# The ring of high and low weight halves in a pool of its own at the other end of the partition

## The chip, the core and the metric

The kernel runs on one core of one Trainium2 chip. The metric is the device time of one execution in microseconds. Kernel and reference take the same inputs, one layer, 512 tokens of width 2048, all in float32.

## The reference, cut to what matters

```python
h = rms_norm(x, norm1_g) * (1.0 + sc1) + sh1        # sc1, sh1, g1, ... = silu(c) @ w_ada + b_ada
proj = h @ w_in                                     # 2048 x 7168
o_hg = hgrn2_mixer(hg_q, hg_f, hg_i, hg_g, ...)     # gated linear recurrence, 8 heads
o_sb = stick_breaking_mixer(sb_q, sb_k, sb_v, ...)  # attention, 8 heads
x = x + g1 * (concatenate([o_hg, o_sb]) @ w_out)    # 2048 x 2048
h = rms_norm(x, norm2_g) * (1.0 + sc2) + sh2
gate, up = split(h @ w_ffn_in, 2)                   # 2048 x 11264
x = x + g2 * ((silu(gate) * up) @ w_ffn_out)        # 5632 x 2048
```

Nearly all of the work is in the four large products with `w_in`, `w_out`, `w_ffn_in` and `w_ffn_out`.

## The kernel before

**Three products for one.** The large products use float32 rounded to a shorter form (`F32R`). To keep float32's accuracy each operand is split into a high half, its rounded copy, and a low half, the rest. A product is then three matmuls: high by high, high by low, low by high (`three`, L227, and the same pattern in `product`, `multiply` and `sb_project`). `split` (L212) makes the halves of a weight piece: ScalarE casts the raw weights into `hi`, VectorE subtracts `hi` from the raw weights into `lo`. Both are put ahead of other work by `tc.high_priority`.

**The ring.** The halves go to tiles of pool `wp` (L137) with the tags `hi` and `lo`, three buffers each, 4096 bytes a partition and buffer: 24,576 bytes in all. The same pool holds `raw`, four buffers of 8192 bytes into which SyncE's queue loads the weights from HBM. In the loop over `w_ffn_in`, and after it, every fourth call of `split` takes its pair of tiles from `spare` instead: `hi2` and `lo2` of pool `tp` in the loop (L1095), a part of tile `opsB` in the last stage (L1156).

**Stages.** The program runs through these, mostly one after the other:

- `st`: the first 1024 columns of `w_in`. The weights are the *moving* operand (512 columns); a piece of `hhi` or `hlo`, the halves of h, is the stationary one that LDWEIGHTS loads. 384 matmuls.
- `sbp`: the attention's projections, 8 heads; weights moving, 384 columns, `hhi` or `hlo` stationary. 8 heads x 8 pieces x 24 = 1536 matmuls. Attention itself is interleaved (`zA`, `tA`, `sbo`, ...).
- `hgf`, `hgq`, `hgg`: the recurrence's projections, 8 heads; weights *stationary* out of the ring, `hhi` or `hlo` moving with 512 columns. 8 x 3 x 48 = 1152 matmuls, with the recurrence between them (`l`, `r`, `hgo`, ...).
- `wo`: the product with `w_out`; weights stationary, 512 columns: 15 x 48 = 720 matmuls, and the last output block in two halves of 256 columns, 96 matmuls.
- `ff`: the first two blocks of `w_ffn_in`, 384 matmuls of 256 columns, beside the second normalisation.
- `ffA`, `ffB`, `ffC`: the loop `for f in range(2, FM)` (L1108), 42 rounds. Each round replaces eight block products by seven (a Strassen-like scheme, with sums of weight blocks made by VectorE), each of 24 matmuls of 256 columns with weights stationary (`product`, L908): 42 x 7 x 24 = 7056 matmuls. A piece `ff_3h` is the high half of the third product's weights out of the ring, `ff_3l` the low half; `ff_3hi` and `ff_3lo` are the same out of the spare pair.
- `foA`, `foB`, `foC`: the product with `w_ffn_out` by the same scheme (`multiply`, L1174); weights moving, 512 columns, 1848 matmuls, of which 1344 take them from the ring and 504 from the spare part of `opsB`.

**Where things lie.** A partition has one address range. Pools on the left side are laid out upwards from its low end, one after another; pools with `side="right"` downwards from its top. A pool that closes frees its stretch for the next. No address is written in the kernel: each follows from the pools that are open.

Of the kernel before, what the change touches and what calls it, by code (L numbers as in the profile page):

```python
# [11 lines left out]
F32R = mybir.dt.float32r  # L12
# [5 lines left out]
P = 128  # L18
# [111 lines left out]
def trunk(ctx, tc, a):  # L130
# [4 lines left out]

    const = ctx.enter_context(tc.tile_pool(name="const", bufs=1))
    wp = ctx.enter_context(tc.tile_pool(name="wp", bufs=3))  # L137
    xctx = ctx.enter_context(ExitStack())
    xop = xctx.enter_context(tc.tile_pool(name="xop", bufs=1, side="right"))
    hp = ctx.enter_context(tc.tile_pool(name="hp", bufs=1))  # L140
# [27 lines left out]
    def small_col(base, i=0):  # L168
        return small[:, base + i:base + i + 1]
# [9 lines left out]
    def gemv(w, row, col):  # L179
        V.scalar_tensor_tensor(w, w, 1.0, row, op0=ALU.mult, op1=ALU.mult, accum_out=col)  # L180

    def finish_gain(comp, k0, k1):
        g, base = (gain1, C_N1) if comp == SC1 else (gain2, C_N2)
        V.scalar_tensor_tensor(g[:, k0:k1], mod[:, comp * KT + k0:comp * KT + k1], 1.0, small[:, base + k0:base + k1],
                               op0=ALU.add, op1=ALU.mult)

    def ada(comp, k):
        j = comp * KT + k
        c = slice(j, j + 1)
        gemv(row_load(a["w_ada"][j], f"ada{j}"), cond, mod[:, c])  # L190
        left[comp] -= 1
        if comp == SC1:
            V.tensor_add(mod[:, c], mod[:, c], small_col(C_BADA, j))
            finish_gain(comp, k, k + 1)
        elif not left[comp]:
            all_k = slice(comp * KT, comp * KT + KT)
            V.tensor_add(mod[:, all_k], mod[:, all_k], small[:, C_BADA + comp * KT:C_BADA + comp * KT + KT])
            if comp == SC2:
                finish_gain(comp, 0, KT)
# [12 lines left out]
    def split(r, shape, name):  # L212
        count[0] += 1
        if spare and count[0] % 4 == 0:
            hi, lo = spare[0](shape, name)
        else:
            hi = wp.tile(shape, F32R, tag="hi", name=name + "h")
            lo = wp.tile(shape, F32R, tag="lo", name=name + "l")
        with tc.high_priority(offset=AHEAD):
            S.copy(hi, r)  # L220
            V.tensor_sub(lo, r, hi.bitcast(F32))
        return hi, lo

    def weights(src, shape, name):
        return split(load(src, shape, name), shape, name)
# [60 lines left out]
    for k in range(KT):  # L286
        xk = xo[:, k]
        if k == 0:
            for i in range(2):
                sl = slice(i * 1024, i * 1024 + 1024)  # L290
                gemv(r0[:, sl], cond[:, sl], lead[:, i:i + 1])
            j = SC1 * KT
            V.scalar_tensor_tensor(mod[:, j:j + 1], lead[:, 0:1], lead[:, 1:2], small_col(C_BADA, j), op0=ALU.add, op1=ALU.add)
            finish_gain(SC1, 0, 1)
            whi = wp.tile([P, 1024], F32R, tag="hi", name="wi0h")
            wlo = wp.tile([P, 1024], F32R, tag="lo", name="wi0l")
            for sl in (slice(0, T), slice(T, 2 * T)):
                S.copy(whi[:, sl], w0[:, sl])
                V.tensor_sub(wlo[:, sl], w0[:, sl], whi[:, sl].bitcast(F32))
        else:  # L300
            nc.sync.dma_start(xk, a["x"][:, k])
            ada(SC1, k)
            if k == 2:
                nc.sync.dma_start(cst, a["cst"])
            if k == KT - 1:
                nc.sync.dma_start(ident2, a["cst"][:, 0])
            whi, wlo = weights(a["w_hi"][k], [P, 1024], f"wi{k}")
        gk = gain1[:, k:k + 1]
        S.activation(hhi[:, k], xk, AF.Identity, scale=gk)
        V.scalar_tensor_tensor(hlo[:, k], xk, gk, hhi[:, k].bitcast(F32), op0=ALU.mult, op1=ALU.subtract)  # L310
        if k == 0:
            S.activation(ss1, xk, AF.Square)
        else:
            sq = sb.tile([P, T], F32, tag="qT" if k % 2 else "kT", name=f"sq{k}", bufs=1)
            S.activation(sq, xk, AF.Square)
            V.tensor_add(ss1, ss1, sq)
        for n in range(2):
            for t in range(4):
                ts_ = slice(t * P, t * P + P)
                cs = slice(n * T, n * T + T)  # L320
                out = banks[n * 4 + t]
                PE.matmul(out, hhi[:, k, ts_], whi[:, cs], start=(k == 0), stop=False)
                PE.matmul(out, hhi[:, k, ts_], wlo[:, cs], start=False, stop=False)
                PE.matmul(out, hlo[:, k, ts_], whi[:, cs], start=False, stop=(k == KT - 1))
# [12 lines left out]
    def sb_project(h):  # L337
        ps = [acc(f"sbp{h}_{t}") for t in range(4)]
        for c in range(8):
            if c % 2 == 0:  # L340
                raw = load(a["w_sb"][h, c // 2], [P, 2, 2, 384], f"wsb{h}_{c}")
            whi, wlo = split(raw[:, c % 2], [P, 2, 384], f"wsb{h}_{c}")
            pairs = [(kk, t) for kk in range(2) for t in range(4)]
            if c in (0, 7):
                pairs.sort(key=lambda p: p[1])
            for kk, t in pairs:
                k = 2 * c + kk
                ts_ = slice(t * P, t * P + P)
                out = ps[t][:, 0:384]
                PE.matmul(out, hhi[:, k, ts_], whi[:, kk], start=(k == 0), stop=False)  # L350
                PE.matmul(out, hhi[:, k, ts_], wlo[:, kk], start=False, stop=False)
                PE.matmul(out, hlo[:, k, ts_], whi[:, kk], start=False, stop=(k == KT - 1))
                clock.run()
        clock.until(lambda: h not in reuse or reuse[h] in done)
        if h in (0, 3):
            rows = scr[:, 0:3].rearrange("p a b -> p (a b)").rearrange("p (t c) -> p t c", t=4)
        else:
            rows = sb.tile([P, 4, 384], F32, tag="rows", name=f"rows{h}")
        for t in range(4):
            if t % 2:  # L360
                V.tensor_copy(rows[:, t], ps[t][:, 0:384])
            else:
                S.copy(rows[:, t], ps[t][:, 0:384])
        ready[h] = rows
# [234 lines left out]
    def mtile(src, name, xhi, xlo, out, nk=KT):  # L599
        n = 0  # L600
        raw = load(src, [P, nk, P], name)
        for c0 in range(0, nk, HALF):
            w = min(HALF, nk - c0)
            whi, wlo = split(raw[:, c0:c0 + w], [P, w, P], f"{name}_{c0}")
            for kk in range(w):
                three(out, whi[:, kk], wlo[:, kk], xhi[:, c0 + kk], xlo[:, c0 + kk], n == 0, n == nk - 1)
                n += 1
                clock.run()
# [734 lines left out]
```

## Time and profile before

| | us |
|---|---|
| median of three runs | 2311.63 |
| lowest and highest run | 2308.95, 2312.49 |
| the profiled execution's own time | 2309.45 |
| its span, first to last instruction | 2307.6 |
| PE busy in the span | 2253.1 (98%), 14171 matmuls |
| DVE busy | 1919.5 (83%) |
| ACT busy | 1160.1 (50%) |

PE is TensorE's matmuls, PEld its weight loads, DVE VectorE, ACT ScalarE, SP the queue that issues the transfers. Matmuls overlap in the records, so a busy PE is not yet a PE at its peak. In the rows of stretches below the columns are length, then busy us (x instructions) of PE, PEld, DVE, ACT and POOL, the granted clock, the DMA engines' busy share and GB/s. What tells more than busy time is the distance from the start of one matmul, or weight load, to the start of the next.

### The profile page before, as it was taken

The page shows a single profiled execution, that of the slowest core. Times are in us where ns is not written, and L with a number is a line of the kernel's source. Part 1 is how long each engine was busy: PE and PEld are TensorE (multiplying, and loading weights), DVE is VectorE, ACT ScalarE, POOL GpSimd, SP SyncE. Part 2 cuts the span into 40 slices and gives each one's busy share as a digit, 9 for nine tenths or more (in the row PEclk, how much of TensorE's full clock was granted, in tenths as well). Part 3 has the DMA queues.
Part 4 walks back from the last instruction along what each step waited for, and adds up shares of the span by engine and source line. Part 5 has one row for each costly group of instructions (what it writes and reads, how often), then busy time and mean ns, then how long its engine had stood idle before and what let it go on. Part 6 is the DMA issues. An engine that isn't in the chain of part 4 may idle for free.

```text
span 2307.6 us, 35720 instructions
## 1 busy us (share of the span) xinstructions
PE 2253.1 (98%) x14171; PEld 2049.8 (89%) x14171; DVE 1919.5 (83%) x2570; ACT 1160.1 (50%) x2011; POOL 10.7 (0%) x25
## 2 busy tenths in 40 slices
PE   8999899999999999989999999999999999999998
PEld 6899799888888788989999999999999978878776
DVE  8887779999887864699899988888888777888888
ACT  4326666565656422654445444454545545454443
POOL 0000000000000000000000000000000000000000
PEclk9999999999999999999999999999999999999999
DMA  9886446843322486336555534454544486654553
GB/s 368 314 319 225 166 153 230 305 170 126 110 92 76 155 294 209 111 114 238 206 203 197 209 133 165 142 174 142 174 142 157 177 343 237 219 178 142 183 204 87
DMA packets 114978, 437.69 MB, mean 190 GB/s; under 512 B 9822, under 2 KB 58236, under 8 KB 76796
## 3 DMA queue, kind: packets, MB, share of 16 engines
q1 hardware_dynamic: 114812, 435.42, 53.0%
q8 instruction: 111, 1.82, 0.3%
q14 instruction: 55, 0.45, 0.1%
HBM read 386.61 MB, written 48.77 MB: 189 GB/s over the span
## 4 chain that ended last, share of the span: by engine, by line
PE 79%; DVE 11%; DMA 4%; ACT 3%; issue 3%; SPq 0%; DVEq 0%; ACTq 0%
PE ffA L93 17%; PE ffC L93 9%; PE foA L93 8%; PE sbp L93 8%; PE wo L93 7%; PE ffB L93 4%; PE foC L93 4%; PE st L93 4%; PE hgf L93 4%; PE hgq L93 3%; PE hgg L93 3%; PE foB L93 1%; DVE ada L180 1%; PE l L93 1%; DMA opd<-fhi 1%
## 5 line engine op out<-in xcount | busy, mean ns | idle before, releaser
L180 DVE SCALAR_TENSOR_TENSOR ada<-ada,cond 128x2048 f32<-128x2048 f32 x95 | 216.9, 2286 | 49.0 <-DMA ada<-in_w_ada 49.0
L93 PE MATMUL ffA<-opD,ff_3h 128*128 128x256 f32 x512 | 93.6, 283 | 0.8 <-ACT u L1008 0.8
L93 PE MATMUL ffA<-opB,ff_6h 128*128 128x256 f32 x512 | 93.6, 283 | 0.2 <-ACT a L1008 0.2
L93 PE MATMUL ffC<-opB,ff_7h 128*128 128x256 f32 x512 | 93.5, 283 | 0.0
L93 PE MATMUL ffC<-opC,ff_4h 128*128 128x256 f32 x496 | 90.8, 284 | 0.4 <-ACT c L1008 0.3
L93 PE MATMUL ffB<-opA,ff_2h 128*128 128x256 f32 x496 | 91.3, 284 | 0.0
L93 PE MATMUL ffA<-opC,ff_5h 128*128 128x256 f32 x496 | 90.6, 283 | 0.0
L93 PE MATMUL ffA<-opA,ff_1h 128*128 128x256 f32 x496 | 90.6, 283 | 0.0
L1082 ACT CAST fhi<-forms 128x512 fp32r<-128x512 f32 (+1 forms) x63 | 43.6, 692 | 90.6 <-DMA opd<-fhi 74.1
L93 PEld LDWEIGHTS ffA<-opD,ff_3h 128*128 128x128 f32 x512 | 79.8, 192 | 1.0 <-ACT u L1008 1.0
L93 PEld LDWEIGHTS ffA<-opB,ff_6h 128*128 128x128 f32 x512 | 79.7, 192 | 0.4 <-ACT a L1008 0.4
L93 PEld LDWEIGHTS ffC<-opB,ff_7h 128*128 128x128 f32 x512 | 79.8, 192 | 0.0
L93 PEld LDWEIGHTS ffC<-opC,ff_4h 128*128 128x128 f32 x496 | 77.2, 192 | 0.8 <-ACT c L1008 0.8
L93 PEld LDWEIGHTS ffB<-opA,ff_2h 128*128 128x128 f32 x496 | 77.7, 193 | 0.1
L93 PEld LDWEIGHTS ffA<-opC,ff_5h 128*128 128x128 f32 x496 | 77.3, 192 | 0.0
L93 PEld LDWEIGHTS ffA<-opA,ff_1h 128*128 128x128 f32 x496 | 77.3, 192 | 0.0
L1083 DVE TENSOR_TENSOR forms<-forms,fhi 128x512 fp32r<-128x512 f32 (+1 forms) x63 | 49.0, 778 | 31.0 <-ACT fhi L1082 30.6
L93 PE MATMUL ffA<-opD,ff_3l 128*128 128x256 f32 x256 | 72.5, 283 | 0.0
L93 PE MATMUL ffC<-opB,ff_7l 128*128 128x256 f32 x256 | 72.4, 283 | 0.0
L93 PE MATMUL ffA<-opB,ff_6l 128*128 128x256 f32 x256 | 72.4, 283 | 0.0
L93 PE MATMUL ffB<-opA,ff_2l 128*128 128x256 f32 x248 | 70.3, 284 | 0.0
L93 PE MATMUL ffA<-opA,ff_1l 128*128 128x256 f32 x248 | 70.2, 283 | 0.0
(1644 smaller groups left out, 7759.3 us busy)
## 6 DMA issues: line engine op xcount, KB each, us to landing
ada<-in_w_ada SPq DMA_DIRECT2D x95, 1024.0 KB, 5.0
wfo<-in_w_fo SPq DMA_DIRECT2D x16, 1024.0 KB, 6.0
yraw<-in_w_fo SPq DMA_DIRECT2D x16, 1024.0 KB, 5.1
fix<-in_w_fix SPq DMA_DIRECT2D x14, 1024.0 KB, 5.7
opsA<-opd SPq DMA_DIRECT2D x12, 1024.0 KB, 4.9
opd<-forms SPq DMA_DIRECT2D x44, 256.0 KB, 3.7
opd<-fhi SPq DMA_DIRECT2D x42, 256.0 KB, 4.2
opd<-forms SPq DMA_DIRECT2D x22, 384.0 KB, 6.7
```

Of the source, the lines that this page charges most:

```text
L93: self.engine.matmul(out, lhsT, rhs, **kw)
L180: V.scalar_tensor_tensor(w, w, 1.0, row, op0=ALU.mult, op1=ALU.mult, accum_out=col)
L1082: S.copy(hi, R[:, q])
L1083: V.tensor_sub(R[:, q].bitcast(F32R), R[:, q], hi.bitcast(F32))
```

## The change

The tags `hi` and `lo` leave pool `wp` for a new pool `wt` with three buffers, on the right side and opened before every other pool there. Nothing else is edited.

```diff
@@ -135,6 +135,7 @@
 
     const = ctx.enter_context(tc.tile_pool(name="const", bufs=1))
     wp = ctx.enter_context(tc.tile_pool(name="wp", bufs=3))
+    wt = ctx.enter_context(tc.tile_pool(name="wt", bufs=3, side="right"))
     xctx = ctx.enter_context(ExitStack())
     xop = xctx.enter_context(tc.tile_pool(name="xop", bufs=1, side="right"))
     hp = ctx.enter_context(tc.tile_pool(name="hp", bufs=1))
@@ -214,8 +215,8 @@
         if spare and count[0] % 4 == 0:
             hi, lo = spare[0](shape, name)
         else:
-            hi = wp.tile(shape, F32R, tag="hi", name=name + "h")
-            lo = wp.tile(shape, F32R, tag="lo", name=name + "l")
+            hi = wt.tile(shape, F32R, tag="hi", name=name + "h")
+            lo = wt.tile(shape, F32R, tag="lo", name=name + "l")
         with tc.high_priority(offset=AHEAD):
             S.copy(hi, r)
             V.tensor_sub(lo, r, hi.bitcast(F32))
@@ -292,8 +293,8 @@
-            whi = wp.tile([P, 1024], F32R, tag="hi", name="wi0h")
-            wlo = wp.tile([P, 1024], F32R, tag="lo", name="wi0l")
+            whi = wt.tile([P, 1024], F32R, tag="hi", name="wi0h")
+            wlo = wt.tile([P, 1024], F32R, tag="lo", name="wi0l")
```

In the built programs every engine has the same instructions in the same order, and each waits for the same semaphores at the same values. Only addresses differ. In bytes from the start of the partition:

| tiles | before | now |
|---|---|---|
| constants, `cond`, `small`, `raw` (11,040 to 43,807) | the same | the same |
| ring: `hi` | 43,808 to 56,095 | 204,768 to 217,055 |
| ring: `lo` | 56,096 to 68,383 | 217,056 to 229,343 |
| `hhi`, `ohi`, `opB`, `opsC` | from 68,384 | from 43,808 |
| `hlo`, `olo`, `opC`, `opsB` | from 101,152 | from 76,576 |
| `opA`, `opsA` (and `cst`) | from 133,920 | from 109,344 |
| `opD` | from 166,688 | from 142,112 |
| spare pair `hi2`, `lo2` | 213,984 to 222,175 | 189,408 to 197,599 |
| every other tile | | 24,576 lower |

## Rows read from the trace of the kernel before

**Rows 1.** The page's first part, TensorE: busy us (share of the span) xinstructions.

```profile
PE 2253.1 (98%) x14171; PEld 2049.8 (89%) x14171; DVE 1919.5 (83%) x2570; ACT 1160.1 (50%) x2011; POOL 10.7 (0%) x25
```

**Rows 2.** Stretches st, sbp, hg, wo, ff, loop, fo: us; busy by engine; clock; DMA.

```profile
11.00:101.00 90.00, 89.46 (x383) 73.67 (x384) 80.47 (x118) 39.16 (x53) 0.00 (x0) 1.00 0.95 357
101.00:438.00 337.00, 326.37 (x1898) 312.39 (x1897) 276.13 (x373) 178.48 (x432) 0.00 (x0) 0.98 0.63 226
438.00:768.00 330.00, 327.62 (x1675) 275.23 (x1674) 288.74 (x541) 201.27 (x444) 9.05 (x16) 1.00 0.36 131
768.00:954.00 186.00, 183.31 (x865) 152.05 (x866) 115.49 (x147) 58.89 (x93) 0.00 (x0) 1.00 0.61 212
954.00:1008.00 54.00, 47.61 (x388) 46.74 (x387) 54.00 (x139) 45.01 (x105) 0.00 (x0) 0.99 0.32 110
1008.00:1848.00 840.00, 836.89 (x7037) 835.83 (x7038) 721.02 (x815) 418.92 (x613) 0.00 (x0) 1.00 0.50 174
1848.00:2307.00 459.00, 441.86 (x1933) 353.87 (x1932) 380.47 (x434) 212.69 (x270) 0.00 (x0) 0.99 0.56 198
```

**Rows 3.** Groups by line, TensorE's matmuls of the loop: xcount, busy us, mean ns.

```profile
L93 PE MATMUL ffA<-opD,ff_3h 128*128 128x256 f32 x512 | 93.6, 283 | 0.8 <-ACT u L1008 0.8
L93 PE MATMUL ffA<-opC,ff_5h 128*128 128x256 f32 x496 | 90.6, 283 | 0.0
...
L93 PE MATMUL ffA<-opC,ff_5l 128*128 128x256 f32 x248 | 70.2, 283 | 0.0
...
L93 PE MATMUL ffA<-opC,ff_5hi 128*128 128x256 f32 x176 | 30.5, 276 | 0.0
```

**Rows 4.** Timeline of weight loads in one round of the loop: start us, us, what.

```profile
1401.04 0.31 PEld L93 LDWEIGHTS ffC<-opB,ff_7hi 128*128 128x128 f32 x2
...
1403.77 0.30 PEld L93 LDWEIGHTS ffA<-opC,ff_5h 128*128 128x128 f32 x2
...
1406.64 0.31 PEld L93 LDWEIGHTS ffC<-opC,ff_4h 128*128 128x128 f32 x2
```

**Rows 5.** Chain of waits in the loop, pieces in order: start us, us, what.

```profile
1204.85 2.88 PE ffA L93 x24
1207.73 2.72 PE ffC L93 x24
```

**Rows 6.** The same view, one piece each of st, sbp, hgq, wo, foA.

```profile
19.78 40.35 PE st L93 x178
...
305.49 4.17 PE sbp L93 x24
...
578.60 2.74 PE hgq L93 x12
...
859.83 30.37 PE wo L93 x134
...
1999.78 7.27 PE foA L93 x32
```

**Rows 7.** Chain shares by line in sbp, hg, wo, the loop and fo.

```profile
by line: PE sbp L93 57.2%; issue 4.8%; PE sbo L93 4.7%; DVE ada L180 4.6%; DVE xo L498 2.8%; DVE fix L180 2.2%; DVE I L440 2.1%; PE zA L93 2.1%; DVE L L434 1.9%; PE qkt L98 1.7%; PE tB L98 1.6%; PE zB L93 1.5%; DVE I L441 1.4%; DVE L L439 0
...
by line: PE hgf L93 25.0%; PE hgq L93 23.2%; PE hgg L93 21.8%; PE l L93 5.8%; PE hgo L93 4.8%; PE r L93 2.8%; issue 2.3%; DMA whg0r<-in_w_hg 2.1%; PE b L93 2.0%; DMA ada<-in_w_ada 1.4%; DVE I L440 0.9%; PE hgo L98 0.8%; DVE ada L180 0.8%; P
...
by line: PE wo L93 87.4%; PE wo15h L93 4.6%; issue 2.3%; PE hgo L93 1.2%; ACT wo_0h L220 0.8%; PE l L93 0.7%; PE r L93 0.7%; ACT x L890 0.6%; DVE wo_8l L221 0.6%; PE ssum L93 0.6%; ACT wo_8h L220 0.6%; PE hgo L98 0.3%; DVE olo L801 0.3%; AC
...
by line: PE ffA L93 47.8%; PE ffC L93 23.9%; PE ffB L93 11.9%; issue 2.8%; DMA opd<-fhi 2.3%; DMA ada<-in_w_ada 1.3%; DMA wu23r<-in_w_fi 0.9%; DMA wu8r<-in_w_fi 0.8%; DMA wu5r<-in_w_fi 0.7%; DMA wu6r<-in_w_fi 0.6%; DMA wu9r<-in_w_fi 0.6%; A
...
by line: PE foA L93 42.0%; PE foC L93 21.7%; PE foB L93 4.7%; DVE yraw L1181 3.7%; issue 3.6%; DVE wfo_2l L221 3.5%; DVE T L1181 3.2%; DVE wfo L1245 2.7%; DVE wfo_0l L221 1.9%; ACT wfo_0h L220 1.8%; DVE wfo L1181 1.7%; DVE opsB L221 1.3%; D
```

**Rows 8.** Groups by line, the writes of the halves: xcount, busy us, mean ns, idle.

```profile
L221 DVE TENSOR_TENSOR ff_5l<-ffS,ff_5h 128x1024 fp32r<-128x1024 f32 x31 | 37.8, 1219 | 0.0
L221 DVE TENSOR_TENSOR ff_5lo<-ffS,ff_5hi 128x1024 fp32r<-128x1024 f32 x11 | 13.4, 1219 | 0.0
```

**Rows 9.** Waits of ScalarE in the loop: who waits for what: us, times, longest.

```profile
ACT fhi L1082 <- DMA opd<-fhi: 74.1, 40, 3.8
```

## The prediction

> **What bounds the kernel now.** First the page's busy times: TensorE works through 98% of the span, VectorE through 83% [rows 1]. Then the same by stage: TensorE is busy 836.89 of 840.00 us in the loop over `w_ffn_in`, 327.62 of 330.00 in the recurrence, 183.31 of 186.00 with `w_out` [rows 2]. Only the stretch `ff` (954 to 1008 us) has another engine full, VectorE with 54.00 of 54.00, and `st` runs at a DMA share of 0.95. The granted clock is 1.00 in nearly every stretch, which is 2.4 GHz. So where the loop, `hg` and `wo` stand, the time is the number of matmuls times the distance from one to the next, and whatever moves that distance moves the end.
>
> The built programs differ in nothing but addresses: the same instructions in the same order on every engine, the same waits. The question is therefore narrow: does the time of any instruction hang on where its operands lie? The kernel before holds a test of that. In the loop three of four weight pieces are read out of the ring, at 43,808 to 68,383, and every fourth out of the spare pair, at 213,984 to 222,175. Shape, type, partner and instruction are the same. The groups by line show a matmul out of the ring at 283 ns and one out of the spare pair at 276 ns, whichever of the halves it reads [rows 3]. A record's length is not its price, since matmuls overlap, so I read starts. In one round the 24 weight loads of a spare product, `ff_7hi` and its low half, go from 1401.04 to 1403.77 us, 2.73 us; the 24 of the ring product `ff_5h` behind it from 1403.77 to 1406.64, 2.87 us [rows 4]. The chain of waits, which in this stretch is TensorE alone, has pieces of 24 at 2.88 us and, for the spare product, at 2.72 us [rows 5]. That is 120.0 and 113.3 ns a matmul: **6.67 ns** between the two places.
>
> How does that come about? In `wo`, 134 matmuls of 512 columns take 30.37 us, 226.6 ns each; in `sbp` 24 of 384 columns take 4.17 us, 173.8 ns [rows 6]. From 256 to 384 to 512 columns the distance grows by 53.8 and 52.8 ns, so 128 columns cost about 53.3 and 256 cost 106.7. Out of the ring 13.3 ns are left over at every width (120.0 - 106.7; 173.8 - 160.0; 226.6 - 213.3), out of the spare pair 6.7. A weight load that came late would be hidden behind a longer stream of columns; the excess isn't. So it is put on the moving stream each time, and half of it goes when the weights lie at the upper end.
>
> **The change part by part.** *Weights out of the ring, 256 columns, the loop.* Three products have 512 + 256 matmuls out of the ring and four have 496 + 248, of which [rows 3] shows one high group of each sort: 3 x 768 + 4 x 744 = 5280, the other 1776 of the 7056 being the spare's. The ring now lies at 204,768 to 229,343, around the stretch where the fast pair lay. 5280 x 6.67 ns = **35.2 us**. Of the chain through this stage TensorE has 47.8 + 23.9 + 11.9 = 83.6% [rows 7]; the rest runs over transfers and other engines that are nearly as late. If only that share is given back, 29.4 us; I take 32. VectorE is next: 721.02 us of then 808 is 89%. ScalarE waits 74.1 us for the writes of `fhi` [rows 9], at most 3.8 us at a time; this stays, and begins to be felt when TensorE is quicker.
>
> *Weights out of the ring, 512 columns.* Nowhere does before have such matmuls out of the upper end. Bounds: 0, if the excess there is of another kind, and 6.67 ns each, from the 256-column rows. I take the upper one since the excess is the same 13.3 ns. `hg`: 8 x 3 x 48 = 1152, 7.7 us, of which 70.0% is on the chain (25.0 + 23.2 + 21.8, [rows 7]), 5.4 us; I take 6.5. `wo`: 720 of 512 columns and 96 of 256, 816 x 6.67 ns = 5.4 us, 92.0% on the chain; I take 5.
>
> *The first two blocks*, `ff`, 384 matmuls, 2.6 us: nothing, VectorE is full there [rows 2]. Were it quicker, they would count.
>
> *The ring as moving operand.* In `st`, `sbp` and `fo` the roles are turned round: the stationary piece is `hhi` or an `ops` tile at the lower end, and stays there, 24,576 lower; the ring's half streams. No row has this with the ring above. If the cost hangs on the pair of places, it is 6.67 ns less here as well; if on the weights' place alone, 0; and in the other direction as much could be lost. `sbp`: 1536 x 6.67 = 10.2 us, 57.2% on the chain, 5.8. `fo`: 1344 x 6.67 = 9.0 us, 42.0 + 21.7 + 4.7 = 68.4% on the chain, 6.2. `st`: 384, 2.6 us, behind a DMA share of 0.95, so 0. Bounds -12.0 and +12.0 us (19.2 if none of it is covered); nearest are the loop's rows with one operand above and one below, which say gain, so I take the half of it, 6.
>
> *The spare pair* moves down to 189,408 to 197,599. The highest place at which stationary pieces are known to be slow is 166,687, where the `ops` tiles end that `fo` multiplies with (7.27 us for 32, 227.2 ns, [rows 6]); the lowest known to be fast is 213,984. If the border lies below 189,408, nothing is lost; if above 197,599, 1776 x 6.67 = 11.8 us, or 9.9 with the share of the chain. I take 0, and keep the loss for the range.
>
> *Casts, subtractions, transfers.* The subtraction that writes a ring half takes 1219 ns, the one that writes a spare half 1219 [rows 8]. Nothing, at either end. Tiles that went down by 24,576 are moving operands between 68,384 and 183,071 in the loop, and 120.0 ns there hold for all of them.
>
> Sum: 32 + 6.5 + 5 + 6 = 49.5 us. The profiled execution took 2309.45 us, so 2260; the median of the runs is 2.2 us above that execution, so **2262 us**.
>
> **The rivals.** *No change.* The Trainium skill, "SBUF — State Buffer", section "SBUF: two separate sides", says that on the engines' side only the port pair that VectorE and GpSimd share makes anyone wait, and that TensorE never waits on anyone; by that a tile's place is free. What the trace has against it is 283 and 276 ns for like matmuls [rows 3]. As a mechanism of this kernel: the 6.67 ns belong to something else that the spare pair has, its single buffer or its own pool, and neither ring nor pair changes. Then 2311.6. For it stands only that place and pool can't be told apart in before.
>
> *The spare pair falls out of the fast stretch*, the ring comes in: 49.5 - 9.9, 2272.
>
> *Only the 256-column stage gains*: 32 us, 2279.6. Against it stands the equal excess at all widths.
>
> *The turned roles lose*: the streaming ring above costs 6.67 ns more, 49.5 - 6 - 12.0 = 31.5, 2280.
>
> *Slower.* What makes weights dear is that ScalarE and VectorE write in the same stretch while they are read. The ring, rewritten for every product, carries that along and gains nothing; the spare pair, whose end is now 7,168 bytes below it, is drawn in: 1776 x 6.67 = 11.8 us more, 2323.4. It decides if that stretch is wider than those bytes. Against it: `wo`, with ScalarE busy 58.89 of 186.00 us, has the same 13.3 ns as the loop with 418.92 of 840.00 [rows 2, 6].
>
> **How the numbers follow.** Forecast (weights gain at both widths, the rest open within its bounds) 0.70; spare pair out 0.13; only 256 columns 0.08; turned roles lose 0.02; no change 0.05; slower 0.02. The best of the forecast, all of 35.2 + 7.7 + 5.4 + 19.2 = 67.5 us, gives 2244; the two middling rivals end at 2280, and with some loss 2282. Range 2244 to 2282. Under 0.2% (4.6 us) this kernel can't be told from no change. Faster 0.93, same 0.05, slower 0.02.
>
> **What would show it.** In the groups by line the `ff` matmuls out of the ring at 276 ns like the spare's, pieces of 24 in the chain at 2.72 us, and the loop some 32 us shorter. `wo` pieces at 219.9 ns a matmul instead of 226.6 show the 512-column step; `sbp` and `foA` pieces below 173.8 and 227.2 the pair of places. A spare group at 283 shows the border between 189,408 and 213,984. If the ring stays at 283 ns, place isn't the cause and the forecast falls; if it reads 276 and the loop still takes 840 us, the chain over `fhi` and the raw loads has taken over.

## The result, and the profile after

The change makes the kernel slower by 0.4%, not faster by 2.1%: 2319.52 us (median of five runs, 2316.51 to 2325.51) against 2311.63, ratio 1.0043 with a 95% interval of 1.0032 to 1.0054. The forecast was 2262, range 2244 to 2282. The profiled execution took 2321.3 us, its span 2319.3.

The first part of the page after, which answers to [rows 1]: VectorE and ScalarE do what they did, TensorE's records add up to 12.8 us more.

```profile
PE 2265.9 (98%) x14171; PEld 2047.2 (88%) x14171; DVE 1921.1 (83%) x2570; ACT 1159.4 (50%) x2011; POOL 10.7 (0%) x25
```

The stretches after, each cut at the first matmul of its stage (us; busy by engine; clock; DMA), as in [rows 2]:

```profile
11.40:103.80 92.40, 92.38 (x384) 74.19 (x385) 80.60 (x116) 38.59 (x52) 0.00 (x0) 1.00 0.92 348
103.80:441.00 337.20, 327.56 (x1894) 313.79 (x1893) 275.27 (x373) 178.45 (x431) 0.00 (x0) 0.98 0.61 226
441.00:773.50 332.50, 329.71 (x1676) 275.72 (x1675) 289.63 (x541) 201.55 (x444) 9.05 (x16) 1.00 0.36 130
773.50:962.30 188.80, 186.12 (x867) 153.14 (x867) 116.34 (x147) 58.95 (x94) 0.00 (x0) 0.99 0.59 208
962.30:1016.50 54.20, 46.85 (x389) 45.91 (x387) 54.20 (x139) 45.19 (x106) 0.00 (x0) 0.98 0.32 110
1016.50:1856.30 839.80, 835.58 (x7057) 833.34 (x7058) 722.33 (x817) 418.81 (x612) 0.00 (x0) 1.00 0.50 175
1856.30:2319.30 463.00, 447.69 (x1914) 351.14 (x1912) 379.06 (x432) 211.65 (x269) 0.00 (x0) 0.99 0.55 194
```

The clock is that of before, 0.98 to 1.00 in every stretch. Cut in the same way, from the first matmul of a stage to the first of the next, the two traces give:

| stage | before, us | after, us | difference | forecast |
|---|---|---|---|---|
| `st` | 89.9 | 92.4 | +2.5 | with `sbp` and `fo` -6 |
| `sbp` | 336.3 | 337.2 | +0.9 | |
| `hg` | 330.1 | 332.5 | +2.4 | -6.5 |
| `wo` | 186.2 | 188.8 | +2.6 | -5 |
| `ff` | 54.1 | 54.2 | +0.1 | 0 |
| loop | 842.1 | 839.8 | -2.3 | -32 |
| `fo` | 457.2 | 463.0 | +5.8 | |

Together +12.0 us; the spans differ by 11.7. The medians differ by 7.9 us only: the profiled execution before took 2.2 us less than its median, the one after 1.8 us more. e2_low_new_offset below, a kernel with the same offsets as the changed one, differs from before by +1.7, +1.1, +2.0, +0.9, +0.1, -4.2 and +5.8 us in these stages, so one execution gives a stage to within some 2 us. Every stage with matmuls of 384 or 512 columns lost, `sbp` by no more than this scatter, and the loop gained a fourteenth of its forecast.

How the loop did that stands in the groups by line after, which answer to [rows 3] (count, busy us, mean ns). Ring and spare pair now read the same, 280 ns: the ring came down from 283, the spare pair went up from 276.

```profile
L93 PE MATMUL ffA<-opD,ff_3h 128*128 128x256 f32 x512 | 92.2, 280 | 1.8 <-ACT u L1009 1.8
L93 PE MATMUL ffA<-opC,ff_5h 128*128 128x256 f32 x496 | 89.1, 280 | 0.5 <-ACT b L1009 0.5
...
L93 PE MATMUL ffA<-opC,ff_5l 128*128 128x256 f32 x248 | 69.3, 279 | 0.0
...
L93 PE MATMUL ffA<-opC,ff_5hi 128*128 128x256 f32 x176 | 31.7, 280 | 0.0
```

The timeline of weight loads in one round after, as in [rows 4] (start us, us, what): 24 loads of the spare product take 1412.03 - 1409.21 = 2.82 us, 24 of the ring product behind it 1414.86 - 1412.03 = 2.83. That is 117.7 ns a matmul for both, where before it was 113.3 and 120.0.

```profile
1409.21 0.30 PEld L93 LDWEIGHTS ffC<-opB,ff_7hi 128*128 128x128 f32 x2
...
1412.03 0.31 PEld L93 LDWEIGHTS ffA<-opC,ff_5h 128*128 128x128 f32 x2
...
1414.86 0.31 PEld L93 LDWEIGHTS ffC<-opC,ff_4h 128*128 128x128 f32 x2
```

5280 x 2.3 ns gained and 1776 x 4.4 ns lost make 12.1 - 7.8 = 4.3 us; 2.1 us of it went into longer waits. Pieces of the chain in other stages after, as in [rows 6]: `st` 86.99 / 369 = 235.7 ns a matmul, waits included (before 226.7), `sbp` 34.36 / 193 = 178.0 (before 173.8), `wo` 131.78 / 574 = 229.6 (before 226.6), `foA` 5.60 / 24 = 233.3 (before 227.2).

```profile
15.62 86.99 PE st L93 x369
...
142.27 34.36 PE sbp L93 x193
...
817.99 131.78 PE wo L93 x574
...
1906.29 5.60 PE foA L93 x24
```

So there are three distances with 256 columns, not two, and one of them, 117.7, the kernel before shows almost nowhere.

### The profile page after: what moved, and what is told of

Read it like the earlier page. It is cut to its first block, busy times and chain, and to the rows that moved or that the text cites. A ratio compares the mean times of both kernels' runs of the same rounds, so it can differ in the third digit from the quotient of the medians.

```text
span 2319.3 us, 35720 instructions
## 1 busy us (share of the span) xinstructions
PE 2265.9 (98%) x14171; PEld 2047.2 (88%) x14171; DVE 1921.1 (83%) x2570; ACT 1159.4 (50%) x2011; POOL 10.7 (0%) x25
## 4 chain that ended last, share of the span: by engine, by line
PE 74%; DVE 15%; DMA 5%; issue 4%; ACT 3%; SPq 0%; DVEq 0%; ACTq 0%
PE ffA L93 15%; PE foA L93 9%; PE sbp L93 8%; PE ffC L93 7%; PE wo L93 7%; PE foC L93 4%; PE st L93 4%; PE ffB L93 4%; PE hgf L93 4%; PE hgq L93 3%; PE hgg L93 3%; DMA opd<-fhi 2%; DMA ada<-in_w_ada 1%; PE foB L93 1%; PE l L93 1%
## 5 line engine op out<-in xcount | busy, mean ns | idle before, releaser
L93 PE MATMUL ffA<-opC,ff_5l 128*128 128x256 f32 x248 | 69.3, 279 | 0.0
```

Source lines behind the costliest of these rows:

```text
L93: self.engine.matmul(out, lhsT, rhs, **kw)
```

## The experiments

The addresses in the table ahead of the prediction have something else in common than their end of the partition. Modulo 256 the ring's is 32 before (43,808 = 171 x 256 + 32) and 224 after (204,768 = 799 x 256 + 224). The spare pair's is 224 in both; `hhi`, `hlo`, `opA` to `opD` and the `ops` tiles have 32 in both. *Offset* below is the address modulo 256. *Weights* are from here on the stationary operand and *columns* the moving one, whatever they hold, and "192 past" means the weights' offset minus the columns', modulo 256. Before, then, the ring was equal to the columns and the spare pair 192 past; after, both are 192 past. In `st`, `sbp` and `fo` the ring is the moving operand, so that there the weights come to stand 64 past.

Three theories went into the first runs: (1) the difference of offsets sets the distance; (2) the place does, as the prediction had it; (3) the writers beside TensorE do.

**m1_alone: TensorE by itself.** Nothing of the reference is computed. One tile of 220 KiB holds finite numbers; each pair of addresses is multiplied 18 times, then the address sequences of both kernels are replayed.

```python
for s, n, w, m in plan():          # set, columns, weights' address, columns' address
    for r in range(18):
        nc.tensor.matmul(out[:, 0:n], big[:, w0:w0 + P], big[:, m0:m0 + n], start=True, stop=True)
```

> The kernel leaves the whole computation out: TensorE alone runs F32R matmuls with the weights and the moving columns read at chosen byte addresses of one large tile, 18 in a row for each pair of addresses, then the loop's, w_out's and the first stage's address sequences as they stand in the kernel before and in the changed one. Theory 1 (the pair of addresses decides, through some bits of both): the sequences alone give back what the two kernels show, 120.0 and 113.3 ns for ring and spare of before, 117.7 for both of after, 226.7 for w_out before and 226 to 232 after; and among the pairs the distance varies with offsets of 32 to 1024 bytes of one operand against the other. Theory 2 (the place alone, far up or low down): the same for the sequences, and in the grid of places a step at one address, whatever the offset. Theory 3 (other engines' reads and writes in the same stretch): with TensorE alone every pair takes the same, 113 ns or less at 256 columns and 220 or less at 512.

Timeline of m1_alone (start us, us, what, count):

```profile
564.84 337.12 PE L86 MATMUL setD<-big 128*128 128x256 f32 x2808
901.80 36.88 PE L86 MATMUL setE<-big 128*128 128x256 f32 x324
938.52 75.75 PE L86 MATMUL setF<-big 128*128 128x512 f32 x324
1014.11 99.21 PE L92 MATMUL setG<-big 128*128 128x256 f32 x576
```

Set D, 156 pairs of places spread over the partition, all at equal offsets: (901.80 - 564.84) / 2808 = 120.0 ns, and no pair outside 119.9 to 120.1. Set E, weights at 18 places, all 192 past: 36.72 / 324 = 113.3. Set F, 512 columns, the columns 192 past the weights, 18 places of the weights: 75.59 / 324 = 233.3. Place does nothing; theory 2 falls. With the weights moved in steps of 32 bytes the distances at 256 columns run through 120.0 (after the first few), 118.1, 113.3, 120.0, 118.5, 119.4, 117.7, 117.8 and repeat with a period of 256. With the columns moved instead, 64 past takes 117.8 and not 113.3. At 512 columns the equal offset is the *best* of them, 226.7, and 192 past takes 228.9. The replayed sequences give the kernels' own distances in `wo`, 226.7 and 228.9, in `st`, 226.7 and 233.3, and in the loop before, 120.0 and 113.3. Two things did not fit theory 1: the loop of the changed kernel, replayed right behind the spare pair of before, took 113.3 for ring and spare pair where the kernel takes 117.7, and 192 past took 113.3 in set E and 117.7 in the sweep.

**m2_with_writers: the same with ScalarE and VectorE writing alongside,** again with nothing of the reference computed.

```diff
+    for i in range(1600):
+        nc.scalar.copy(ra, raw)
+    for i in range(2400):
+        nc.vector.tensor_sub(rd, raw[:, 0:T // 2], raw[:, T // 2:T])
```

> As m1_alone, with ScalarE casting 128x512 and VectorE subtracting 128x256 without a pause beside the matmuls, into a stretch that no matmul reads. Theories 1 and 2: every distance as in m1_alone, within 1 ns. Theory 3: distances rise, by 6 ns or more, while the two other engines run, and not in all pairs alike.

Replayed: 120.00 and 113.34 for ring and spare pair of before, 226.67 and 228.91 for `wo`, 226.67 and 233.33 for `st`, as in m1_alone; ScalarE's copies ended at 1080 us, so beside the replay of `st` only VectorE wrote. Theory 3 falls for writers as such. They write here to tiles that no matmul reads; writers in the same stretch as the weights, as in the prediction's rival, are left to e1.

**e1 and e2: the offset exchanged in the real kernels.** e1_top_old_offset is the changed kernel with the ring's offset put back to 32; the second pad keeps the spare pair at 224. The other tiles of the right side move by 192 bytes as well. e2_low_new_offset is the kernel before with the ring's offset at 224.

```diff
# e1_top_old_offset, against the changed kernel
+    rp0 = ctx.enter_context(tc.tile_pool(name="rp0", bufs=1, side="right"))
+    rp0.tile([P, 48], F32, name="rp0t")
     wt = ctx.enter_context(tc.tile_pool(name="wt", bufs=3, side="right"))
...
+    tq = tctx.enter_context(tc.tile_pool(name="tq", bufs=1, side="right"))
+    tq.tile([P, 16], F32, name="tqt")
     tp = tctx.enter_context(tc.tile_pool(name="tp", bufs=2, side="right", reuse_waits="tile"))
# e2_low_new_offset, against the kernel before
+    lp0 = ctx.enter_context(tc.tile_pool(name="lp0", bufs=1))
+    lp0.tile([P, 48], F32, name="lp0t")
     wp = ctx.enter_context(tc.tile_pool(name="wp", bufs=3))
...
+    lp1 = ctx.enter_context(tc.tile_pool(name="lp1", bufs=1))
+    lp1.tile([P, 16], F32, name="lp1t")
     hp = ctx.enter_context(tc.tile_pool(name="hp", bufs=1))
```

> The changed kernel with the ring still at the upper end, but its whole right side lowered by 192 bytes, so that the ring lies 32 bytes past a multiple of 256 as it did before the change (it was 224 past one in the changed kernel), and the spare pair 64 bytes lower again, so that it stays 224 past one. Instructions and waits are those of both kernels. Theory 1 (the offset between weights and columns within 256 bytes sets the distance): the time is that of the kernel before, 2311.6 us within 3; in the loop ring products stand 120.0 ns apart and spare ones 113.3, wo 226.7, st 226.7. Theory 2 (the upper end itself): as the changed kernel, 2319.5 within 3, ring and spare 117.7. Theory 3 (the order in which pools are laid out moves some other buffer that matters): neither pattern, or the pattern of the changed kernel in some stages alone.

> The kernel before with the ring at its old, lower end, but 192 bytes higher, so that it lies 224 bytes past a multiple of 256, as in the changed kernel; everything behind it is moved by 256 bytes, which leaves its offset as it was. Theory 1 (offset): the time is that of the changed kernel, 2319.5 us within 3; loop products of ring and spare 117.7 ns apart, wo 229, st 233.3. Theory 2 (the upper end itself): as the kernel before, 2311.6 within 3, with 120.0 and 113.3.

e1: 2310.43 us, ratio to before 1.0001 (0.9992 to 1.0009). The groups by line, and two pieces of 24 from the chain of waits, show the ring slow and the spare pair quick again, at the upper end:

```profile
L93 PE MATMUL ffA<-opC,ff_5h 128*128 128x256 f32 x496 | 90.9, 284 | 0.2 <-ACT b L1013 0.2
...
L93 PE MATMUL ffA<-opC,ff_5hi 128*128 128x256 f32 x176 | 30.8, 277 | 0.6 <-ACT b L1013 0.6
...
1240.34 2.88 PE ffA L93 x24
1243.22 2.72 PE ffC L93 x24
```

e2: 2319.82 us, ratio 1.0040 (1.0027 to 1.0053). The same views show the picture of after, at the lower end:

```profile
L93 PE MATMUL ffA<-opC,ff_5h 128*128 128x256 f32 x496 | 89.0, 279 | 0.0
...
L93 PE MATMUL ffA<-opC,ff_5hi 128*128 128x256 f32 x176 | 31.6, 279 | 0.0
...
1204.41 2.83 PE ffA L93 x24
1207.23 2.83 PE ffC L93 x24
```

The other widths go along: by the starts, without waits, `st` takes 226.7 ns in e1 and 233.3 in e2, `wo` 227.1 and 229.0, and before and after 226.7 and 233.3, 227.0 and 229.0. The writes of ScalarE and VectorE lie in e1 where they lie in the changed kernel but for 192 or 256 bytes, so they are not the cause either.

192 bytes give the whole difference and the other end of the partition gives none of it. For the question of the prediction that is the answer. What stays is why the same offsets take 113.3 in one kernel and 117.7 in another, and what the quick one is worth.

**e4 and e5: the ring 64 past.** In the sweep 64 past took 113.3. Both start from the kernel before and move the loop's operands by 192 bytes inside widened tiles, which leaves the other stages as they were; e5 also lowers the spare pair by 192.

```diff
+    def padded(pool, tag, name, shift):
+        t = pool.tile([P, 2 * HALF * 2 * HT + 64], F32R, tag=tag, name=name)
+        return t[:, shift:shift + 2 * HALF * 2 * HT]
...
-    late = hp.tile([P, 2, HALF, 2, HT], F32R, tag="hhi", name="opB")
+    late = padded(hp, "hhi", "opB", 48).rearrange("p (a j s t) -> p a j s t", a=2, j=HALF, s=2)
# opC alike; opA begins 48 words into a widened tile, which moves opD behind it too; every other tile of these tags begins at 0
```

> The kernel before with the loop's operands (opA, opB, opC, opD) 192 bytes higher, so that ring weights lie 64 bytes past the columns' place within 256 bytes and the spare pair, a quarter of the products, lies equal to it. The stages with 384 and 512 columns keep their equal offsets. Theory 1 with the distances of the first micro run (64 past: 113.3, equal: 120.0): 5292 ring matmuls save 6.67 ns each, 35.3 us, 1764 spare ones lose 6.67, 11.8 us; 2311.6 - 23.5 = 2288 us. If 64 past has a slow pace too (117.7, as 192 past had in the changed kernel): 2311.6 - 12.2 + 11.8 = 2311. Theory 2 (the upper end alone): 2311.6.

> As e4_ring64_spare0, with the spare pair 192 bytes lower too, so that all weights of the loop lie 64 bytes past the columns' place within 256 bytes and no product stands at equal offsets. If 64 past holds 113.3 ns by itself: 5292 x 6.67 = 35.3 us less, 2276 us. If it holds 113.3 only where a product at equal offsets ran just before, it falls to about 117.7 in all 7056 matmuls: 2311.6 - 12.2 + 7.8 = 2307 us. Theory 2 (the upper end alone): 2311.6.

e4: 2309.91 us, ratio 0.9989 (0.9979 to 0.9999). e5: 2305.68, ratio 0.9979 (0.9971 to 0.9988). Neither came near the lower number. In e4 the ring products behind a spare product at equal offsets, where no wait lay between, ran at 117.7 in all 67 places, so from equal offsets to 64 past the quick pace isn't reached. The timeline of e5 (start us, us, what, count, idle before) shows two products at the very same offsets:

```profile
1344.00 0.50 PE L93 MATMUL ffA<-opC,ff_5hi 128*128 128x256 f32 x2 [0.90 <-ACT b L1014]
...
1344.45 0.39 PE L93 MATMUL ffA<-opC,ff_5hi 128*128 128x256 f32 x2
...
1346.49 0.39 PE L93 MATMUL ffA<-opC,ff_5hi 128*128 128x256 f32 x2
...
1347.35 0.50 PE L93 MATMUL ffC<-opC,ff_4h 128*128 128x256 f32 x2 [0.35 <-ACT c L1014]
...
1347.81 0.40 PE L93 MATMUL ffC<-opC,ff_4h 128*128 128x256 f32 x2
...
1349.57 0.40 PE L93 MATMUL ffC<-opC,ff_4h 128*128 128x256 f32 x2
```

Between 1344.45 and 1346.49 lie 18 matmuls, 113.3 ns each; then TensorE waits for ScalarE's copy `c`; between 1347.81 and 1349.57 lie 15, 117.3 each. Through the whole loop the pace changes only at such waits and is kept from one to the next: 102 of the 294 products ran at 113.3, 190 at 117.7, and the last 78, behind the last wait, all at 117.7.

**e6, e7 and m3: how a stretch begins.** In the kernel before a spare product always follows ring products at equal offsets, and 72 of them ran at 113.3. e6_lock_each_seventh puts ring and spare pair 192 past, and leaves the first product of each `f` at equal offsets by its columns; e7_no_lock moves that one too. m3_how_a_stretch_begins computes nothing of the reference; it runs each offset behind products at equal offsets, and behind waits.

```diff
# e6: the first half of opA stays at equal offsets; opB, opC, opD as in e4 with 16 words for 48; spare pair 192 bytes lower
-    early = fh.tile([P, 2, HALF, 2, HT], F32R, tag="b1", name="opA")
+    early = fh.tile([P, 4 * HALF * HT + 16], F32R, tag="b1", name="opA")
+    early = [early[:, i:i + 2 * HALF * HT].rearrange("p (j s t) -> p j s t", j=HALF, s=2) for i in (0, 2 * HALF * HT + 16)]
# e7: ... for i in (16, 2 * HALF * HT + 16)]
```

> The kernel before with the loop's weights (ring and spare) 192 bytes past the columns' place within 256 bytes in six of the seven products; the first product of each f (operand opA, first half) keeps equal offsets. Theory 1a (one pair of offsets has two paces; which one holds is set where a stretch begins, a product at equal offsets just before sets 113.3 ns, a wait sets either, and it stays until the next wait): 1008 matmuls at 120.0, 6048 near 113.3; against before 1764 at 113.3 and 5292 at 120.0, so (5292 - 1008) x 6.67 = 28.6 us less, 2282 us, some us more for stretches that a wait has set slow until the next first product. Theory 1b (the pace at 192 past goes with something else in the loop, such as the casts that run beside it): about 117.7 in the six products as in the changed kernel, 2311.6 - 12.2 + 7.8 + 1008 x 2.3 = 2309 us.

> As e6_lock_each_seventh, but the first product's operand is moved by 64 bytes too, so that no product of the loop stands at equal offsets. Theory 1a: nothing sets the fast pace any more, stretches after a wait are fast or slow by chance, mostly slow as in the changed kernel: 2300 to 2308 us, loop about 840. Theory 1b: as e6, less 1008 x 2.3 = 2.3 us.

> No part of the reference's computation is done; TensorE multiplies blocks of one 96 KiB buffer. For 256, 384 and 512 columns, 24 products at equal offsets stand ahead of 48 products at each offset from 0 to 240 bytes in steps of 16; then, for each offset in steps of 32, 30 products come twelve times after a wait for VectorE of 1 to 12 copies; then offsets 192 and 64 after 24 products at 160 and 1 to 24 at 0. Theory 1a: at 256 columns, 192 past runs at 113.3 ns every time after products at equal offsets and at 113.3 or 117.7 after a wait; 64 past does not always take 113.3. At 384 and 512 columns the equal offset (173.3, 226.7) stays the fastest. Theory 1b: each offset has one pace, however it is entered, since nothing else runs here.

e6: 2311.02 us, ratio 0.9999 (0.9990 to 1.0008); e7: 2310.00, ratio 0.9995 (0.9986 to 1.0004). Theory 1a missed e6: none of its products ran at 113.3. Each product at equal offsets ran at 120.0, and the one behind it fell straight to 117.7, 41 times of 41 (in one round the distances go 120, 120, 122, 117, 119, 117, 118). It missed e7 too, by 2 us against its 2300 to 2308; 18 products there ran at 113.3. m3 shows that the step does work with TensorE alone, as in the kernel before. Its timeline: 24 products at equal offsets (`setA`), then 48 with the weights 176, 192 and 208 past (`setB`):

```profile
117.35 5.83 PE L72 MATMUL setB<-big 128*128 128x256 f32 x48
123.02 3.04 PE L72 MATMUL setA<-big 128*128 128x256 f32 x24
125.90 5.60 PE L72 MATMUL setB<-big 128*128 128x256 f32 x48
131.34 3.04 PE L72 MATMUL setA<-big 128*128 128x256 f32 x24
134.22 5.77 PE L72 MATMUL setB<-big 128*128 128x256 f32 x48
```

(131.34 - 125.90) / 48 = 113.3 for 192 past, and of the sixteen offsets it is the only one: the others run from 116.6 to 120.1, 64 past at 117.8. Behind a wait, 192 past took 117.8 in all eight pieces that did wait; 64 past took 113.3 in three of six. So one pair of offsets has two paces with no other work beside it, and theory 1b falls. At 384 columns eight offsets, the equal one among them, take 173.3, the others 175.6 to 177.4; at 512 columns 0, 16, 144 and 240 take 226.7, the others 228.9 to 234.3. That is the changed kernel's own picture: where its ring streams, the stationary tile is 64 past it, which costs 176.7 at 384 columns and 233.3 at 512. Two limits of the run: the scheduler laid pieces of later sets between the waits, so that not every piece of the twelve had one, and the question of how many products at equal offsets are enough got no clean answer.

In the kernel before and in m3 the *weights* step from equal to 192 past while the columns stay; in e6 the columns step. That is theory 1c for the next runs.

**e8, e9 and e10: the spare pair as the lock.** A *lock* is a product at equal offsets that leaves the quick pace to the products behind it. Every fourth product takes its weights from the spare pair. Put that at equal offsets and the ring 192 past, and the step is one of the weights. e8_after_spare_equal is the changed kernel with nothing but 192 bytes ahead of `tp`; e9 and e10 are low-end kernels in which the other stages keep equal offsets.

```diff
# e8, against the changed kernel
+    tq = tctx.enter_context(tc.tile_pool(name="tq", bufs=1, side="right"))
+    tq.tile([P, 48], F32, name="tqt")
# e9, against e7
-    tq.tile([P, 48], F32, name="tqt")
+    tq.tile([P, 32], F32, name="tqt")
# e10: the loop's operands 64 bytes on as in e7, lp0 as in e2, tq as in e8
```

> The changed kernel with one thing moved: the spare pair 192 bytes lower, so that its weights, a quarter of the loop's products, stand at equal offsets with the columns; the ring stays at the upper end and 192 past, so nothing else differs from the changed kernel. Theory 1c (a step of the weights alone from equal to 192 past carries the fast pace along, as ring to spare did 72 times in the kernel before; a step of the columns alone, as in e6, does not): 5292 ring matmuls fall from 117.7 to 113.3, 23.3 us, 1764 spare ones rise from 117.7 to 120.0, 4.1 us: 2319.5 - 19.2 = 2300 us, loop about 820 us. If no lock holds over three products: 2319.5 + 4.1 = 2324 us.

> As e7_no_lock, with the spare pair 64 bytes higher, so that it stands at equal offsets with the loop's columns (all 96 past a multiple of 256) while the ring is 192 past them; the stages with 384 and 512 columns keep equal offsets. Theory 1c, if only the difference of the two offsets counts: loop 7056 matmuls of which 5292 at 113.3 and 1764 at 120.0, against before the other way round: 3528 x 6.67 = 23.5 us less, 2287 us. If the absolute offsets count (columns at 96 instead of 32), as e7, about 2310 to 2314.

> The same design as e9 with the very offsets of the kernel before in the loop: ring 224, loop's columns 32, spare 32 past a multiple of 256, and hhi, hlo and the operands of the last stage at 224 like the ring, so that the stages with 384 and 512 columns keep equal offsets. Theory 1c: 2287 us whether the difference or the absolute offsets count. If products at equal offsets do not carry the pace over three ring products: 2310 to 2315.

The lock holds: of 220 ring products 176 (e8), 171 (e9) and 180 (e10) ran at 113.3, and where no wait lay between, the product behind the spare one reached it in 58 of 59, 56 of 59 and 58 of 60 places. The time did not follow: e8 2316.18 us (ratio 1.0026, 1.0016 to 1.0037), e9 2306.50 (0.9981, 0.9972 to 0.9990), e10 2304.90 (0.9974, 0.9964 to 0.9984). The chain of waits of e10 has both halves of this (start us, us, what):

```profile
1265.83 4.81 DMA opd<-fhi
...
1270.71 0.62 ACT fhi L1090
1271.33 0.28 ACT u L1016
...
1271.65 5.92 PE ffA L93 x48
1277.57 2.87 PE ffB L93 x24
1280.45 2.72 PE ffA L93 x24
1283.17 2.72 PE ffC L93 x24
1285.89 2.72 PE ffA L93 x24
1288.61 2.88 PE ffC L93 x24
```

Three ring products of four in 2.72 us, the spare one in 2.88; and ahead of them TensorE waits for the tap copy `u`, which stands behind the cast into `fhi` in ScalarE's order, which waits until transfers have emptied the only `fhi` buffer. By the loop's starts the mean distance without a wait falls from 118.34 to 115.55 ns, 7056 x 2.79 = 19.7 us, while the waits, counted over 120 ns each, grow from 7.1 to 20.0 us. The loop gets 6.4 us shorter, from 842.0 to 835.6 between its first and last matmul. (The 24.9 us in the next expectation is the difference of the two sums of such distances; 46 of them have become waits, so it is some 5 us too much.)

**e11 and e12: a second `fhi` buffer.** The loop leaves some 3 KiB of a partition free between `opD` and `forms`.

```diff
-                hi = tp.tile([P, b - a, HT], F32R, tag="fhi", name=f"fhi{f}_{a}", bufs=1)
+                hi = tp.tile([P, b - a, HT], F32R, tag="fhi", name=f"fhi{f}_{a}", bufs=2)
```

> e10_same_offsets_low with a second fhi buffer (it lies in 3 KiB that the loop leaves free); the scheduler then puts some DVE and ACT work of the loop in another order, TensorE's order is the same. In e10 the distances inside the loop's products came to 24.9 us less than before, while its waits grew from 7.1 to 20.0 us over the pace and the whole time fell by 5.7 us only. Theory A (ScalarE, which works in order, waits for the DMAs that empty the one fhi buffer, 99.5 us in e10, and the tap copies queued behind it hold TensorE): the waits fall back to about 8 us, 2304.9 - 12 = 2293 us. Theory B (VectorE and ScalarE have no work time to spare at this pace): waits stay near 20 us, 2305.

> The kernel before with a second fhi buffer and nothing else. The loop's waits in the kernel before come to 7.1 us over the pace, 6.2 of them the first. Theories A and B alike: the same time as before within 3 us, 2308 to 2312; so what e11 gains on e10 comes from the waits that the faster pace brought.

e11: **2288.24 us**, ratio 0.9901 (0.9886 to 0.9916), the best of all these kernels. e12: 2306.45, ratio 0.9977 (0.9967 to 0.9986), below the 2308 to 2312 that both theories had given it. The waits in the loop (us, times, longest), first e10, then e11:

```profile
PE ffA L93 <- ACT u L1016: 6.3, 6, 2.5
...
ACT fhi L1090 <- DMA opd<-fhi: 99.5, 41, 5.1
```

```profile
PE ffA L93 <- ACT u L1016: 2.9, 2, 2.2
...
ACT fhi L1090 <- DMA opd<-fhi: 22.4, 19, 2.9
```

The waits over the pace fall from 20.0 to 9.0 us, and with fewer of them the lock is lost less often: 215 of 220 ring products at 113.3. Theory A holds, though no run separates the buffer from the new order in which the scheduler puts some of VectorE's and ScalarE's work with it. More came than its 12 us: 7056 x (118.34 - 115.06) = 23.1 us by the pace, less 1.9 for waits, against 21.1 measured in the loop. The buffer is worth 5.2 us by itself, the offsets 5.7 by themselves, both together 23.4. In e12 ScalarE's wait for the one buffer falls from 74.1 to 20.4 us and TensorE's waits in the loop from 7.1 to 3.4. ("6.2 of them the first" in its expectation is a misreading: that wait, for `sg`, lies ahead of the loop's first matmul and isn't among the 7.1, which could therefore shrink.)

| kernel | ring / spare pair, past the columns in the loop | mean ns without wait | loop, us | waits, us | ratio to before |
|---|---|---|---|---|---|
| before | 0 / 192 | 118.34 | 842.0 | 7.1 | 1 |
| after | 192 / 192 | 117.70 | 839.7 | 9.2 | 1.0043 |
| e5 | 64 / 64 | 116.24 | 839.0 | 18.6 | 0.9979 |
| e7 | 192 / 192 | 117.48 | 837.1 | 8.2 | 0.9995 |
| e8 | 192 / 0 | 115.60 | 838.7 | 22.8 | 1.0026 |
| e10 | 192 / 0 | 115.55 | 835.6 | 20.0 | 0.9974 |
| e11, two `fhi` | 192 / 0 | 115.06 | 820.9 | 9.0 | 0.9901 |
| e12, two `fhi` | 0 / 192 | 118.35 | 838.4 | 3.4 | 0.9977 |

(Distances of up to 125 ns count as without wait; the longer ones, each less 120 ns, are the waits. One execution each.) The column of waits also holds matmuls at the lower clock: behind the wait of 6.2 us at the loop's start in `before` the granted clock is 0.50, which is 1.2 GHz, and 26 matmuls take 5.80 us; behind a wait of 2.75 us at 1151 us in e10 15 of them stand some 213 ns apart. Such matmuls are 2.1 of the 7.1 us before, 2.7 of the 20.0 in e10 and 2.1 of the 9.0 in e11.

```profile
1008.20:1014.00 5.80, 5.80 (x26) 5.75 (x27) 5.80 (x8) 1.82 (x4) 0.00 (x0) 0.50 0.54 181
```

## Why the prediction was wrong, point by point

**The step that failed** is the second paragraph's: "6.67 ns between the two places". The rows were read rightly, 120.0 and 113.3, and m1_alone gives the same two numbers. The cause was not place. Ring and spare pair differed in place, pool, number of buffers and in the low byte of their address; the prediction weighed the first three and never looked at the fourth, though every address needed for it stood in its table. e1 and e2 settle it in both directions. Neither of the signs that the prediction had named came: the ring's group reads 280 ns, neither 276 nor 283.

**The excess that is the same at all widths.** 13.3 ns over 53.3 per 128 columns was right: m3 has 120.0, 173.3 and 226.7 at equal offsets. That half of it would go at every width was not. At 512 columns no offset tried was below 226.7, at 384 none below 173.3, so there the kernel before already stood at the best, and a move could only lose or change nothing. This turns `hg` from -6.5 to +2.4, `wo` from -5 to +2.6, and the three stages with the ring as moving operand from -6 to +9.2. The bounds of that last term, -12.0 to +12.0, held the result; the value taken from them had the wrong sign.

**The loop's term, 32 us,** measured -2.3. Two things went wrong in it. The ring came to 192 past and so left the worst distance, but only for 117.7, because nothing ahead of it stands at equal offsets any more. And the spare pair, "take 0, and keep the loss for the range", lost 4.4 ns on 1776 matmuls, 7.8 us of the 11.8 that the range had kept, not for a border between places but because its predecessor, the ring at equal offsets, was gone.

**The cover behind the loop was also too thin.** The prediction gave back 32 of 35.2 us and said of ScalarE's wait for `fhi` [rows 9] that it "begins to be felt when TensorE is quicker". e10 took 19.7 us out of TensorE's distances and got 6.4: that wait grew from 74.1 to 99.5 us and came onto the chain. e10 and e11 suggest that even with the right cause the loop with one `fhi` buffer would have given far less than 32; the 74.1 us were the row to price.

**Casts and subtractions at no cost** held: VectorE's busy time is 1919.5 and 1921.1 us [rows 1].

**The rivals.** "No change" rested on the Trainium skill, "SBUF — State Buffer", section "SBUF: two separate sides", which says that TensorE never waits on anyone; that a tile's place is then free is what the prediction made of it. As to place the runs agree: 156 pairs of places, 119.9 to 120.1 ns. The sentence gives no price to the offset between TensorE's own two operands, and there 0.4% of this kernel lay. "Slower" had the right side and about the right size, 2323.4, with the wrong mechanism, which is luck: e1 leaves the writers where they are and takes the time of before, 2310.43 us, and the spare pair lost 4.4 ns and not 6.67. "The turned roles lose", with a chance of 0.02, was right in its own part, 226.7 to 233.3 ns in `st`, but not by place, since e2, with the ring at the low end, takes 233.3 too; its time, 2280, failed with the gain of the rest. The chances were at fault too. Place, pool and buffer count could not be told apart in before, as the prediction says itself, and yet a forecast that needed one of them, and needed it at every width, got 0.70.

**What stays open.** Why the distance goes with the offsets, and why a step of the weights carries the pace of 113.3 along and a step of the columns does not, no run here shows. e11's lock costs a quarter of the products 6.67 ns each; a shorter one wasn't tried.

## What to carry to other kernels

When two like instructions differ in pace, list everything in which their operands differ, the low byte of the address too, before one difference is named the cause: a cause read off one pair is a guess. A change of pools moves such offsets without a word in the diff, so compare addresses modulo 256 of weights and columns before and after. And where the bounding engine gets quicker, price the longest wait of the in-order engines beside it: here a second 3 KiB buffer turned 5.7 us of gain into 23.4.

## What the runs showed of the hardware that was not expected

- With float32r operands the distance of back-to-back matmuls follows the difference of the byte addresses of weights and columns modulo 256, not the place: 113.3 to 120.1 ns at 256 columns, 173.3 to 177.4 at 384, 226.7 to 234.3 at 512. Equal offsets are among the dearest at 256 columns (120.0) and the cheapest at 384 and 512.
- One pair of offsets can have two paces at 256 columns, 113.3 and 117.7 ns, and keeps one until TensorE waits; behind a wait either can follow. Seen at 64 past (e5: 102 products at 113.3, 190 at 117.7) and 192 past. Weights that step from equal to 192 past take 113.3 in nearly every case without a wait (72 products of the kernel before, 176, 171 and 180 of 220 in e8 to e10); columns that make the step don't (none in e6).
- ScalarE's and VectorE's writes beside TensorE, to tiles that no matmul reads, did not change any of these distances (m2_with_writers: 120.00, 113.34, 226.67, 228.91, 233.33).
